# Low parts of split weights: an accumulating DMA onto the negated high parts in place of a subtraction on VectorE or GpSimd

## The chip, the core and the metric

The kernel runs as one program on one core of a Trainium2 chip. The metric is the device time of one execution in microseconds (us). Five engines work side by side, each through its own queue of instructions in order: TensorE (PE; its weight loads are shown as PEld), VectorE (DVE), ScalarE (ACT), GpSimd (POOL) and SyncE (SP). DMAs are issued from the queues of SP, ACT and POOL and are carried by 16 DMA engines, which all of them share.

## The reference, cut to what matters

The model is a trunk of four sublayers in each of two layers, on 512 tokens of 1024 features in float32. Everything that is heavy is a product of activations with a weight matrix from DRAM:

```
for i in range(DEPTH):                       # DEPTH = 2
    x = layer_norm(DN_ALPHA * x + 0.5 * swiglu_ffn(x, ffn1_wgu[i], ffn1_wd[i]), ...)
    mix = mlstm_mixer(...) if i % 2 == 0 else gmlp_mixer(...)
    x = layer_norm(DN_ALPHA * x + mix, ...)
    x = layer_norm(DN_ALPHA * x + 0.5 * swiglu_ffn(x, ffn2_wgu[i], ffn2_wd[i]), ...)
    ple = jax.nn.sigmoid(x @ ple_wg[i] + ple_bg[i]) * (p[i] @ ple_wp[i])
    x = layer_norm(DN_ALPHA * x + ple, ...)

def swiglu_ffn(x, w_gu, w_d):                # w_gu [1024, 2*2816], w_d [2816, 1024]
    g, u = jnp.split(x @ w_gu, 2, axis=-1)
    return (jax.nn.silu(g) * u) @ w_d
```

## The kernel before

Each float32 operand of a product is written as the sum of two float32r numbers of 12 significand bits, a high part and a low part. A product is then three matmuls (`mm3`, L150 to L154): high by high, high by low, low by high. Activations are split where they are made (`split`, L156 to L158, and `turn_x`).

Weights come in tiles of 128 partitions by 1024 elements, 512 KB each, 396 of them in one execution. The class `Weights` streams them in the order of use. `load` (L78) brings one or two tiles by a DMA from SP into one of three raw buffers (`wraw`, 1 MB each). `fill` takes the next tile in the order for which a pair of buffers is free, writes its high part `whi` with a ScalarE copy that rounds (L96), and its low part `wlo = wraw - whi` with a subtraction (L97) on VectorE, or on GpSimd where the caller asked for it (`low=pool`). `take` hands the next tile to a product; `release`, written where the last product of a tile is, frees the buffers and at once writes the splits of the tile that will take them. Held tiles (`later=True`) are freed by `refill`.

There are six pairs of split buffers ("main"), and in some stages four more ("rows"), so a tile's split stands some five or six tiles ahead of its use. In several places it stands closer: where four tiles are used in turn by every block of tokens (`up_tokens`: the values of the mLSTM, the second half of the gMLP's input, the gate of the input embedding, here called PLE), a group's tiles are all released within its last block of tokens, and the next group needs its own four within one block.

Tiles come in three forms. Most (for the FFN's first matrix, q, k, z and the gMLP's u) are 8 blocks of rows by 128 columns, so a tile's partition is 8 runs of 512 B in DRAM and, because two tiles share a raw buffer, in the raw buffer too. Tiles of the down projections are whole rows of 1024 elements; those of `up_tokens` are two rows of 512 elements.

The order of the work is written out by hand (`manual_schedule`): each engine runs its instructions in the order in which the code emits them, and waits by semaphores for its operands and for its output buffer. GpSimd's own work, beside the splits that it is given, is small: a power in each LayerNorm (L375), half of the norm's scale and shift (L381, L382), masks, and a power in the mLSTM (L730) and the gMLP (L836).

Of the kernel before, what the change touches and what calls it, by code (L numbers as in the profile page):

```python
# [9 lines left out]
F32 = mybir.dt.float32  # L10
F32R = mybir.dt.float32r
AF = mybir.ActivationFunctionType
OP = mybir.AluOpType
PSUM = bass.MemoryType.PSUM
DRAM = bass.MemoryType.DRAM

P = 128
# [20 lines left out]

# Weights are split on chip into two float32r parts (12 significand bits each, their sum is exact).
RAW_BUFS = 3  # L40
# [3 lines left out]
class Weights:  # L44
    """Streams weight tiles through SBUF in the order of use: a DMA brings one or two tiles, each of
    which is split into its high and low part ahead of its use, as soon as a tile is released."""

# [10 lines left out]
    def add(self, *loads, kind="main"):  # L58
        """Each (ap, views): ap [128, a, b] of DRAM, at most 2048 elements a partition; the views are
        the tiles in it. The tiles of several loads take turns."""  # L60
        first = len(self.loads)
        self.loads.extend(ap for ap, _ in loads)
        self.left.extend(len(views) for _, views in loads)
        for i in range(len(loads[0][1])):
            self.order.extend((first + j, views[i], kind) for j, (_, views) in enumerate(loads))
# [16 lines left out]
    def fill(self, most=1000, low=None):  # L82
        while most and self.next_split < len(self.order):
# [10 lines left out]
            for i in range(parts):  # L94
                s = slice(i * shape[1] // parts, (i + 1) * shape[1] // parts)
                self.nc.scalar.activation(hi[:, s], raw[:, s], AF.Copy)  # L96
                (low or self.nc.vector).tensor_sub(lo[:, s], raw[:, s], hi[:, s].bitcast(F32))  # L97
            self.ready.append((hi, lo))
# [12 lines left out]
    def release(self, n=1, kind="main", later=False, low=None):  # L111
        """The last products of n tiles are emitted. later: their successors' splits wait for refill().
        low: the engine for the low part."""
        if later:
            self.held.extend([kind] * n)
        else:
            self.free[kind] += n
            self.fill(low=low)
# [12 lines left out]
def hybrid_trunk(ctx: ExitStack, tc, x, p, ln_g, ln_b, ffn1_wgu, ffn1_wd, ffn2_wgu, ffn2_wd,  # L131
# [18 lines left out]
    def mm3(ps, st, mv, start, stop):  # L150
        """ps += st.T @ mv with both operands in two parts."""
        mm(ps, st[0], mv[0], start=start, stop=False)  # L152
        mm(ps, st[0], mv[1], start=False, stop=False)  # L153
        mm(ps, st[1], mv[0], start=False, stop=stop)  # L154
# [14 lines left out]
    def row_ap(src, offset, n):  # L169
        """n contiguous elements of DRAM on all partitions."""  # L170
        return bass.AP(tensor=src.tensor, offset=src.offset + offset, ap=[[0, P], [1, n]])

    # ---- the order of the weights
    W = Weights(nc, raw_pool, split_pool)
# [10 lines left out]
    def add_pairs(w, a0, b0):  # L185
        """Two tiles of columns from a0 and two from b0, in turns."""
        W.add((w_cols(w, a0), cols2), (w_cols(w, b0), cols2))
# [5 lines left out]
    def add_wide(w, c0, kind="main"):  # L193
        """Four tiles, each two blocks of rows of 512 columns."""
        for k in (0, 4):
            W.add((kp(w)[:, k:k + 4, c0:c0 + 512], half4), kind=kind)
# [60 lines left out]

    # ---- the input, by tokens and by features
    xt = act.tile([P, TB, D], F32, name="xt")
# [17 lines left out]
    def turn_x(t, bank=dn_bank, halves=(0, 1)):  # L277
        """A block of tokens by features, in two parts."""
        for g in halves:
# [7 lines left out]

    # ---- parameters by feature: one column for each block of 128 features
    NCOL = 160
# [33 lines left out]

    # both parts of the gates' weights side by side, the bias for the first
    G = 2 * HEADS
# [6 lines left out]
    def load_gates():  # L332
# [9 lines left out]
        vec.memset(all_ones, 1.0)  # L342
        # tri[s, t] = 1 for s <= t
        pool.affine_select(out=tri, in_=all_ones, pattern=[[1, P]], compare_op=OP.is_ge, fill=0.0, base=0,
# [6 lines left out]

    # ---- LayerNorm over the features, by tokens and in place
    class Norm:
# [8 lines left out]
        def stats(self, t, i, n):  # L362
            """Of the i-th of n parts of the features."""
            if i == 0:
                self.st[t] = small.tile([P, n, 6], F32, name="st", tag=f"st{n}")
            vec.bn_stats(self.st[t][:, i], xt[:, t, i * D // n:(i + 1) * D // n])  # L366

        def apply(self, t, shared=False):
            """shared: GpSimd takes a half of the features."""
            y = xt[:, t]  # L370
# [26 lines left out]

    # what is left of a norm, for the next stage to run between its first products
    hooks = []
# [13 lines left out]
    def down(hs, first, norm=None, kind="main", low=None):  # L413
        """Adds hs.T @ (the next tiles of weights) to the residual, a block of tokens after the other."""
        n = len(hs)
        ws = []
# [26 lines left out]
    def up(ps, w, t0=0, t1=SEQ, hooked=()):  # L443
        """ps = w.T @ x for some tokens, by features."""
        for kb in range(KB):
# [4 lines left out]
    def up_staged():  # L450
        """The same for three tiles of weights, by tokens as they come."""
        banks = [up_bank("sup") for _ in range(3)]
# [8 lines left out]
    def up_tokens(t, ws, ps, c=slice(0, 512), hook=None, release=None):  # L461
        """ps = x @ w for a block of tokens, with four tiles of two blocks of rows each."""
        for kb in range(KB):
# [10 lines left out]

    # ---- macaron half-step: x = LN(alpha x + 0.5 swiglu(x))
    def ffn(layer, k, prepare=None):
# [36 lines left out]

    # ---- mLSTM over the whole sequence: the state's sums written out
    def mlstm():
        b_in = ml_b_in
        with tc.tile_pool(name="ml", bufs=1) as mp:
            rows_d = dram.tile([HEADS, SEQ], F32, name="rows_d")
            # by tokens: i_s + (sum of log f from s to the end of the d-th block before the target's), exp(-m)
            reach = mp.tile([P, 4, TB, HEADS], F32, name="reach")  # L520
# [18 lines left out]
            def gate_logs():  # L539
# [7 lines left out]
                vec.tensor_add(fg, ps[:, :, HEADS:G], low[:, :, HEADS:])  # L547
                # log sigmoid(f) = min(f, 0) - log(1 + e), e = exp(-|f|); log(1 + e) = 2 atanh(e / (2 + e))
                vec.scalar_tensor_tensor(e, fg, -1.0, fg, op0=OP.mult, op1=OP.max)
# [13 lines left out]
            def gate_sums():  # L563
                """Sums of log f within a block of tokens (up to each token, and whole), the rows of i and log f."""
                ps = dn_bank("gsum")
# [20 lines left out]
            def gate_rows():  # L586
                """By target, for all sources alike: the sum of log f from its block's start less the maximum."""
                brow, mcol = up_bank("brow"), dn_bank("mcol")
# [14 lines left out]
            def project_qk(h):  # L603
                """q and k by features, after the convolution over tokens."""
                qh, ql = big("A", F32R, "qh"), big("B", F32R, "ql")
# [38 lines left out]
            def project_v(h, vb, between=()):  # L644
                """v by tokens, with two columns of ones between its halves."""
                ws = []
# [14 lines left out]
            def project_z(h, sz, i):  # L661
                """norm_g sigmoid(z), a block of features."""
                ps = up_bank("zps")
# [12 lines left out]
            def scores(h, qk, rt):  # L676
                """(q k) exp(...) by source, in blocks of sources."""
                qh, ql = qk
# [22 lines left out]
            def mix(h, ss, v):  # L701
                vh, vl = v
                hn = big("A", F32, "hn")
                for t in reversed(range(TB)):
                    bank = up_bank if t >= 2 else dn_bank
                    pa, pb = bank("nps"), bank("nps")
                    for j in range(t + 1):
# [8 lines left out]
                        mm(pb[:, :HV], sl[:, s], vh[:, j, HV + 2:], start=False, stop=last)  # L716
                    # h = num / max(|den|, exp(-m)); its LayerNorm from the sums of num
                    r = small.tile([P, 6], F32, name="hr", tag="hr")
# [60 lines left out]

    # ---- gMLP: gating by a product over the tokens of a block  # L780
    def gmlp():
        with tc.tile_pool(name="gm", bufs=1) as mp, tc.tile_pool(name="ghpool", bufs=4) as hpool:
            vf = mp.tile([P, TB, GW], F32, name="gvf")
            # both parts of a group's weights side by side
            wsp = mp.tile([P, GRP, 2, P], F32R, name="wsp")
# [6 lines left out]
            def spatial_weights():  # L792
# [3 lines left out]
                for a in range(2):  # L796
# [6 lines left out]
                    vec.tensor_sub(wsl[:, s], ps, wsh[:, s].bitcast(F32))  # L803
                # the later half of a block's tokens is hidden from the earlier
                vec.memset(wsh[64:128, :, 0:64].bitcast(F32), 0.0)
# [53 lines left out]
            def spatial(b, v):  # L859
                """The gate of a block of features: vn_g * P + (vn_b * rowsum(ws) + bs)."""  # L860
                vh, vl = v
# [44 lines left out]

    # ---- gated input embedding: x = LN(alpha x + sigmoid(x wg + bg) * (p wp))
    def ffn_ple(i, last):
# [116 lines left out]
```

## Time and profile before

| | |
|---|---|
| median of 2 runs | 2328.59 us (2328.36 to 2328.81) |
| span of the profiled execution | 2324.9 us, 3.7 us below that median |
| ACT busy | 699.2 us, 30% of the span |
| DMA, mean over the span | 98 GB/s |
| HBM read | 224.51 MB |
| weight loads of 1 MB from `ffn_wgu` | 80, median 5.8 us to landing |

The profile is of one execution. "Busy" is the time in which an engine had an instruction running. Groups of instructions are listed by source line with their count, total and mean time, and the idle time of their engine just before them with what ended it. The share of a DMA queue is the time of its packets as a share of 16 engines over the span.

### The profile page before, as it was taken

Reading aid. Unit: us, or ns where it says so; the run is one execution under the profiler, and the core shown is the slowest. Engines: PE = TensorE matmul, PEld = TensorE weight load, DVE = VectorE, ACT = ScalarE, POOL = GpSimd, SP = SyncE. Lnnn points to the kernel's source line nnn. Section 1 sums busy time; section 2 is a strip of 40 time slices with the busy share of each in tenths; the row PEclk is TensorE's granted clock in tenths of the full one; section 3 lists DMA queues with packets and bytes.
Section 4 is the critical chain, followed back from the end, with each engine's and each line's share of the span. In section 5 each row is a group of like instructions: output and inputs, shape, how many; then the busy total and the mean of one; then the engine's idle time right before and its main releaser. Section 6 shows DMA issues by size and latency. Waiting matters only on the chain. (4 is left out here: it accounts for less than half of the span.)

```text
span 2324.9 us, 25736 instructions
## 1 busy us (share of the span) xinstructions
PE 2286.6 (98%) x10814; PEld 1910.0 (82%) x10814; DVE 1250.3 (54%) x1753; ACT 699.2 (30%) x936; POOL 268.1 (12%) x187
## 2 busy tenths in 40 slices
PE   8999999999999999999999999999999999999998
PEld 7888888887878788888888888888888888888887
DVE  5433347686666753434477434336566584333467
ACT  4222222443534142222233222222333333222222
POOL 1000003122242400000021000002021230000022
PEclk9999999999999999999999999999999999999999
DMA  6333231132231233333222332231322234322411
GB/s 201 127 109 104 74 112 42 59 118 92 81 100 55 100 109 109 109 109 127 82 91 91 127 109 91 82 118 50 122 91 94 76 121 140 96 95 69 145 46 55
DMA packets 164140, 228.26 MB, mean 98 GB/s; under 512 B 4277, under 2 KB 130325, under 8 KB 164025
## 3 DMA queue, kind: packets, MB, share of 16 engines
q1 hardware_dynamic: 157120, 211.83, 27.7%
q10 hardware_dynamic: 6616, 14.69, 2.1%
q8 instruction: 84, 1.38, 0.2%
q14 instruction: 32, 0.25, 0.0%
q0 software_dynamic: 288, 0.12, 0.0%
HBM read 224.51 MB, written 2.11 MB: 97 GB/s over the span
## 5 line engine op out<-in xcount | busy, mean ns | idle before, releaser
L97 DVE TENSOR_TENSOR wlo<-wraw,whi 128x1024 fp32r<-128x1024 f32 (+1 forms) x342 | 412.8, 1232 | 355.2 <-ACT whi L96 352.4
L154 PE MATMUL fps<-xh,wlo 128*128 128x512 f32 x1312 | 510.9, 389 | 0.0
L153 PE MATMUL fps<-xl,whi 128*128 128x512 f32 x1312 | 510.8, 389 | 0.0
L152 PE MATMUL fps<-xh,whi 128*128 128x512 f32 x1312 | 510.6, 389 | 0.0
L96 ACT ACTIVATE whi<-wraw 128x1024 fp32r<-128x1024 f32 (+1 forms) x397 | 406.0, 1048 | 235.5 <-PE dps L154 181.9
L153 PE MATMUL dps<-wlo,hh 128*128 128x512 f32 x960 | 375.8, 391 | 6.5 <-DVE wlo L97 6.5
L154 PE MATMUL dps<-whi,hl 128*128 128x512 f32 x960 | 376.1, 392 | 2.7 <-DVE hl L158 2.7
L152 PE MATMUL dps<-whi,hh 128*128 128x512 f32 x960 | 377.4, 393 | 0.3 <-ACT hh L157 0.3
L153 PEld LDWEIGHTS fps<-xl,whi 128*128 128x128 f32 x1312 | 246.3, 188 | 51.5
L152 PEld LDWEIGHTS fps<-xh,whi 128*128 128x128 f32 x1312 | 246.3, 188 | 51.4
L154 PEld LDWEIGHTS fps<-xh,wlo 128*128 128x128 f32 x1312 | 246.3, 188 | 51.2
L396 DVE TENSOR_TENSOR xt<-xt,dps 128x512 f32<-128x512 f32 x208 | 141.1, 683 | 250.6 <-PE dps L154 250.4
L153 PEld LDWEIGHTS dps<-wlo,hh 128*128 128x128 f32 x960 | 180.3, 188 | 46.7 <-DVE wlo L97 8.3
L154 PEld LDWEIGHTS dps<-whi,hl 128*128 128x128 f32 x960 | 180.2, 188 | 42.7 <-DVE hl L158 3.6
L152 PEld LDWEIGHTS dps<-whi,hh 128*128 128x128 f32 x960 | 180.3, 188 | 38.8 <-ACT hh L157 0.5
L497 ACT ACTIVATE sg<-fps 128x512 f32<-128x512 f32 x80 | 47.4, 593 | 504.7 <-PE fps L154 504.7
L375 POOL TENSOR_TENSOR rs<-rs,eps_pow 128x1 f32<-128x1 f32 x32 | 21.1, 659 | 1519.7 <-DVE rs L374 1519.7
L97 POOL TENSOR_TENSOR wlo<-wraw,whi 128x1024 fp32r<-128x1024 f32 x55 | 143.3, 2614 | 260.4 <-ACT whi L96 229.4
L157 ACT ACTIVATE hh<-hf 128x512 fp32r<-128x512 f32 x88 | 55.7, 633 | 339.8 <-DVE hf L500 337.9
L500 DVE SCALAR_TENSOR_TENSOR hf<-sg,fps 128x512 f32<-128x512 f32 x84 | 57.6, 685 | 167.8 <-PE fps L154 167.8
L158 DVE TENSOR_TENSOR hl<-hf,hh 128x512 fp32r<-128x512 f32 x88 | 60.9, 692 | 61.5 <-ACT hh L157 61.5
L285 ACT ACTIVATE xh<-xps 128x512 fp32r<-128x512 f32 x64 | 37.4, 595 | 146.9 <-PE xps L283 146.9
(237 smaller groups left out, 2961.0 us busy)
## 6 DMA issues: line engine op xcount, KB each, us to landing
wraw<-in_ffn_wgu_dram SPq DMA_DIRECT2D x80, 1024.0 KB, 5.8
wraw<-in_ffn_wd_dram SPq DMA_DIRECT2D x44, 1024.0 KB, 4.9
wraw<-in_ml_w_in_dram SPq DMA_DIRECT2D x24, 1024.0 KB, 5.5
wraw<-in_gm_w_in_dram SPq DMA_DIRECT2D x15, 1024.0 KB, 5.7
wraw<-in_ml_w_out_dram SPq DMA_DIRECT2D x8, 1024.0 KB, 4.9
wraw<-in_ple_wg_dram SPq DMA_DIRECT2D x8, 1024.0 KB, 5.1
wraw<-in_gm_w_out_dram SPq DMA_DIRECT2D x8, 1024.0 KB, 4.9
wraw<-in_ffn_wgu_dram SPq DMA_DIRECT2D x15, 512.0 KB, 4.2
```

The source lines that it names most:

```text
L96: self.nc.scalar.activation(hi[:, s], raw[:, s], AF.Copy)
L97: (low or self.nc.vector).tensor_sub(lo[:, s], raw[:, s], hi[:, s].bitcast(F32))
L152: mm(ps, st[0], mv[0], start=start, stop=False)
L153: mm(ps, st[0], mv[1], start=False, stop=False)
L154: mm(ps, st[1], mv[0], start=False, stop=stop)
L157: sca.activation(hi, src, AF.Copy)
L158: vec.tensor_sub(lo, src, hi.bitcast(F32))
L285: sca.activation(xh[dst], ps, AF.Copy)
L375: pool.tensor_tensor(rs[:, 1:2], rs[:, 0:1], eps_pow, op=OP.pow)
L396: vec.tensor_add(dst, dst, ps)
L497: sca.activation(sg, pg, AF.Silu)
L500: vec.scalar_tensor_tensor(hf, sg, 0.5, pu, op0=OP.mult, op1=OP.mult)
```

## The change

The first two tiles are split as before. For every later tile the subtraction is gone. ScalarE copies the raw tile a second time, with a scale of -1, into `wlo`, so that `wlo` holds minus the rounded high part. Then GpSimd issues a DMA that adds the raw float32 tile onto `wlo`; the DMA reads the raw values, reads what is in `wlo`, adds, and writes `wlo`. For tiles with an even number the raw values are read from the raw buffer in SBUF; for tiles with an odd number they are read a second time from DRAM. The argument `low` no longer has an effect for these tiles. Comments and docstrings are removed as well, and the lines below the edit move down by five.

```
                 self.nc.scalar.activation(hi[:, s], raw[:, s], AF.Copy)
-                (low or self.nc.vector).tensor_sub(lo[:, s], raw[:, s], hi[:, s].bitcast(F32))
+                if self.next_split < 2:
+                    self.nc.vector.tensor_sub(lo[:, s], raw[:, s], hi[:, s].bitcast(F32))
+                else:
+                    self.nc.scalar.activation(lo[:, s], raw[:, s], AF.Copy, scale=-1.0)
+                    src = self.loads[j][view] if self.next_split % 2 else raw[:, s]
+                    self.nc.gpsimd.dma_start(lo[:, s], src, accum_op=OP.add)
```

394 of the 396 tiles take the new way. 214 of them have 8 runs of 512 B in a partition, the others one or two longer ones. Three places show what this does to the order on the engines; the numbers behind the names tell buffers apart.

ScalarE near the start, after the first tokens are turned (`xh`), before:

```order
L285 ACTIVATE xh_84<-xps_232 128x4x128
L96 ACTIVATE whi_251<-wraw_95 128x1024
L96 ACTIVATE whi_255<-wraw_129 128x1024
L96 ACTIVATE whi_259<-wraw_95 128x1024
L96 ACTIVATE whi_265<-wraw_129 128x1024
L96 ACTIVATE whi_271<-wraw_149 128x1024
```

and the same place in the changed kernel:

```order
L290 ACTIVATE xh_84<-xps_232 128x4x128
L96 ACTIVATE whi_251<-wraw_95 128x1024
L100 ACTIVATE wlo_252<-wraw_95 128x1024
L96 ACTIVATE whi_256<-wraw_129 128x1024
L100 ACTIVATE wlo_257<-wraw_129 128x1024
L96 ACTIVATE whi_261<-wraw_95 128x1024
L100 ACTIVATE wlo_262<-wraw_95 128x1024
```

Each high part is now followed by the negated copy, so a burst of splits is twice as long on ScalarE.

VectorE in the PLE of the first layer, where two buffers of weights and four of the second half's tiles come free together; `pg` is the gate's sum, the first work behind the splits, before:

```order
L286 TENSOR_TENSOR xl_85<-xps_8722,xh_84 128x4x128
L97 TENSOR_TENSOR wlo_8730<-wraw_8297,whi_8729 128x1024
L97 TENSOR_TENSOR wlo_8734<-wraw_8297,whi_8733 128x1024
L97 TENSOR_TENSOR wlo_8740<-wraw_8365,whi_8739 128x1024
L97 TENSOR_TENSOR wlo_8744<-wraw_8365,whi_8743 128x1024
L97 TENSOR_TENSOR wlo_8750<-wraw_8433,whi_8749 128x1024
L97 TENSOR_TENSOR wlo_8756<-wraw_8737,whi_8755 128x1024
L966 TENSOR_TENSOR pg_8790<-gps_8765,bgb_8634 128x512
```

and GpSimd at the same place in the changed kernel, between the last power of the norm before and the first of the norm behind:

```order
L380 TENSOR_TENSOR rs_8819<-rs_8819,eps_pow_102 128x1
L102 DMA wlo_8930<-wraw_8493 128x1024
L102 DMA wlo_8935<-in_ple_wg_dram 128x2x512
L102 DMA wlo_8942<-wraw_8563 128x1024
L102 DMA wlo_8947<-in_ple_wg_dram 128x2x512
L102 DMA wlo_8954<-wraw_8633 128x1024
L102 DMA wlo_8961<-in_ffn1_wgu_dram 128x8x128
L380 TENSOR_TENSOR rs_9036<-rs_9036,eps_pow_102 128x1
```

Six subtractions leave VectorE, and six DMA issues stand on GpSimd's queue ahead of the next norm's power.

SP's queue in the first FFN, where raw buffers are loaded, with what each issue waits for (DMAHW are earlier DMAs of SP, DMASW are DMAs of GpSimd), before:

```order
L78 DMA wraw<-in_ffn_wgu_dram 128x8x256 [waits DMAHW7_49,DVE_49]
L78 DMA wraw<-in_ffn_wgu_dram 128x8x256 [waits DMAHW3_49,DMAHW0_49,DVE_49]
L78 DMA wraw<-in_ffn_wgu_dram 128x8x256 [waits DMAHW1_49,DVE_49]
L78 DMA wraw<-in_ffn_wgu_dram 128x8x256 [waits DMAHW5_49,DMAHW2_49,DVE_49]
L78 DMA wraw<-in_ffn_wd_dram 128x2x1024 [waits DMAHW6_49,DMAHW3_49,DVE_49]
```

and in the changed kernel:

```order
L78 DMA wraw<-in_ffn_wgu_dram 128x8x256 [waits DMAHW0_49,Activation_49]
L78 DMA wraw<-in_ffn_wgu_dram 128x8x256 [waits DMAHW3_49,DMAHW7_49,DMASW3_49,DMASW1_49]
L78 DMA wraw<-in_ffn_wgu_dram 128x8x256 [waits DMAHW1_49,DMASW5_49,Activation_49]
L78 DMA wraw<-in_ffn_wgu_dram 128x8x256 [waits DMAHW2_49,DMASW7_49,DMAHW5_49,DMASW1_49,Activation_49]
L78 DMA wraw<-in_ffn_wd_dram 128x2x1024 [waits DMAHW6_49,DMAHW3_49,Activation_49]
```

A raw buffer was free once VectorE had subtracted; now it is free once ScalarE has copied and, where the tile's DMA reads the buffer, once that DMA has landed.

## The prediction

> **What bounds the kernel now.** I read the page's busy times first, then who waits for whom, then the busy times by stretch, and last the timeline at the places where a weight tile is split late.
>
> ```profile
> span 2324.9 us, 25736 instructions
> PE 2286.6 (98%) x10814; PEld 1910.0 (82%) x10814; DVE 1250.3 (54%) x1753; ACT 699.2 (30%) x936; POOL 268.1 (12%) x187
> L97 DVE TENSOR_TENSOR wlo<-wraw,whi 128x1024 fp32r<-128x1024 f32 (+1 forms) x342 | 412.8, 1232 | 355.2 <-ACT whi L96 352.4
> L96 ACT ACTIVATE whi<-wraw 128x1024 fp32r<-128x1024 f32 (+1 forms) x397 | 406.0, 1048 | 235.5 <-PE dps L154 181.9
> L97 POOL TENSOR_TENSOR wlo<-wraw,whi 128x1024 fp32r<-128x1024 f32 x55 | 143.3, 2614 | 260.4 <-ACT whi L96 229.4
> ```
>
> PE has work for 2286.6 of 2324.9 us: only 38 us could be won by any change that leaves the matmuls alone. The subtractions that the change removes (412.8 us on DVE, 143.3 us on POOL) lie on engines that are half idle or more. What PE waits for among them is in the view of waits:
>
> ```profile
> PE dps L153 <- DVE wlo L97: 6.5, 4, 1.8
> PE sup L154 <- DVE wlo L97: 0.8, 1, 0.8
> SPq L78 <- DVE wlo L97: 1782.7, 173, 53.3
> ```
>
> PE waits 7.3 us in all for low parts, and SP stands 1782.7 us waiting for raw buffers to come free: weights arrive far ahead, and the splits keep up. So the change can win almost nothing, and the question is whether the new way to a low part keeps up too: in rate, over a whole FFN, and in latency, where a tile is split shortly before its use.
>
> **The rate.** The third FFN has 66 tiles, and its stretch is this (time, then busy time of PE, PEld, DVE, ACT and POOL, the clock, DMA share and GB/s):
>
> ```profile
> 1250.00:1593.00 343.00, 343.00 (x1545) 284.95 (x1544) 147.44 (x166) 94.13 (x115) 3.89 (x3) 1.00 0.34 111
> q1 hardware_dynamic: 252, 0.97, 12.5%
> ```
>
> PE uses a tile in 343/66 = 5.2 us and never idles. The DMA engines spend 0.34 x 343 = 117 us, which is 1.77 us of all 16 engines on each tile of 512 KB. The second row is the queue of loads in a 20 us stretch with one burst of long rows: 0.97 MB for 2.5 us of all engines, or 1.35 us a tile. One pass of 512 KB thus costs 1.35 to 1.77 us. An accumulating DMA is nowhere in the trace. It cannot cost less than a plain pass, and by its work (it reads the raw values, reads `wlo`, writes `wlo`) I bound it at three passes. I take two, one for each operand read, because a plain pass already holds a read and a write side by side: 2.7 to 3.5 us. With the raw load, a tile then takes 4.05 to 5.3 us of the DMA engines against PE's 5.2 us. It fits, barely. I use 4.7 us as the spacing of low parts in a burst.
>
> The Trainium skill, "Collectives: The Full Stack", section "Why ReduceScatter is half of AllGather", says that an add in the DMA engines costs nothing by itself, and that the second source read halves the rate, from about 31 GB/s an engine. No run here shows it. By its figure, as an estimate, an accumulation of 512 KB takes 2.1 us and a tile 3.5 us, no FFN would be short of DMA, and the sum below would be about 2379 us instead of the forecast.
>
> **The change part by part.** ACT gets 394 more copies of 1.05 us (the row of L96 above), 413 us in all: 699 + 413 = 1112 us, 48% of the span. That is hidden in rate, but each negated copy stands behind its high part and delays it, as below. DVE loses 410 us, POOL loses 143 us of subtraction; nobody waits long for either, so I count 0 (at most the 7.3 us). POOL gets 394 DMA issues. The nearest rows are the loads that POOL issues at the start:
>
> ```profile
> 5.20 0.95 POOL L335 DMA_DIRECT2D graw<-in_ml_w_in_dram  x1
> graw<-in_ml_w_in_dram POOLq DMA_DIRECT2D x1, 32.0 KB, 7.0
> gbias<-in_ml_b_in_dram POOLq DMA_DIRECT2D x1, 0.0 KB, 5.1
> wraw<-in_ffn_wgu_dram SPq DMA_DIRECT2D x80, 1024.0 KB, 5.8
> wraw<-in_ffn_wgu_dram SPq DMA_DIRECT2D x15, 512.0 KB, 4.2
> ```
>
> `graw` has 1024 runs, as many as a tile of columns, and takes 0.95 us to issue. I take 1.0 us a tile, at most 1.9 if the second read is written as well: 394 to 750 us of 2325, hidden beside PE. What is queued behind an issue on POOL is the norm's power (L375). At the one stage end that matters (the last block of tokens of the mLSTM and gMLP) POOL does a subtraction of 2.6 us in the same place today, so 0.
>
> The landing time is what counts. 512 KB from SP land in 4.2 us; small loads from POOL took 5.1 to 7.0 us, among the start's other loads. I take 4.2 plus one more pass, 6.0 us; the ends are 4.2 (as a plain load) and 7.0 + 1.8 = 8.8. From the start of the high part to a usable low part: 2 x 1.05 + 1.0 + 6.0 = 9.1 us, where today it is 1.05 + 1.23 = 2.3 us. For most tiles 9.1 us is covered by the five tiles of 5.2 us that PE has in hand. The cover is thin in these places; each pair of rows is the high part's start and the first matmul that needs its low part:
>
> ```profile
> 20.09 5.80 ACT L96 ACTIVATE whi<-wraw 128x1024 fp32r<-128x1024 f32 x6
> 22.46 0.39 PE L154 MATMUL sup<-xh,wlo 128*128 128x256 f32 x1 [0.76 <-DVE wlo L97]
> 491.40 1.05 ACT L96 ACTIVATE whi<-wraw 128x1024 fp32r<-128x1024 f32 x1
> 495.78 0.39 PE L153 MATMUL vps<-wlo,xh 128*128 128x512 f32 x1
> 1188.27 4.84 ACT L96 ACTIVATE whi<-wraw 128x1024 fp32r<-128x1024 f32 x5
> 1193.24 0.40 PE L153 MATMUL gps<-wlo,xh 128*128 128x512 f32 x1
> 1194.65 0.39 PE L153 MATMUL gps<-wlo,xh 128*128 128x512 f32 x1
> 1234.58 1.05 ACT L96 ACTIVATE whi<-wraw 128x1024 fp32r<-128x1024 f32 x1
> 1240.93 0.28 PE L154 MATMUL sup<-xh,wlo 128*128 128x256 f32 x1
> 1624.30 1.06 ACT L96 ACTIVATE whi<-wraw 128x1024 fp32r<-128x1024 f32 x1
> 1625.66 1.06 ACT L96 ACTIVATE whi<-wraw 128x1024 fp32r<-128x1024 f32 x1 [0.30 <-PE gvps L154]
> 1631.13 0.39 PE L153 MATMUL gvps<-wlo,xh 128*128 128x512 f32 x1
> ```
>
> - Start, third tile: 20.09 + 9.1 = 29.2 against 22.46: 6.7 us.
> - Values of the mLSTM, fourth tile of the first head: 500.5 against 495.78: 4.7 us; two later heads have about 4 us more room: 0.6 each. Together 6 us.
> - PLE, second half of the gate: 1197.4 against 1193.24: 4.1 us; PE takes a new tile every 1.41 us there (1194.65 - 1193.24), and the next three low parts come 4.7 us apart: 3 x 3.3 = 9.9. Two layers: 28 us.
> - First FFN tile behind that PLE: 1243.7 against 1240.93: 3 us.
> - gMLP, the two tiles split in a group's last block of tokens: 1633.4 against 1631.13: 2.3 us, and 4.7 - 1.36 = 3.3 for the second. Three changes of group: 17 us.
>
> That is 61 us. On top comes the rate: 0 if a tile takes 4.05 us of DMA, and at 5.3 us 264 FFN tiles x 0.1 = 26 us, plus 28 us for the 16 loads of norm parameters (1.77 us each) that then find no gap. Because 214 of the accumulations are cut into runs of 512 B, I lean to the upper end and take 45 of these 54 us. Sum: 2324.9 + 61 + 45 = 2431; the median of the runs stands 3.7 us above the span: 2435 us.
>
> **The rivals.** *Three passes or more: DMA becomes the bound.* A tile takes 5.4 to 7.1 us of DMA. For: short runs, and a destination that must be read, changed and written. Against: nothing in the trace. Price: 264 FFN tiles x 0.2 to 1.9 us, at the middle 277 us; about 20 us in the gMLP (48 tiles in 300 us); the thin places with a chain of 10.6 and a spacing of 6.2 us cost 8 + 10 + 40 + 4 + 26 = 88 us. 2324.9 + 385 + 3.7 = 2714 us, from 2500 to 2960. PE would wait for low parts in the middle of each FFN.
>
> *The DMA is hidden: not slower.* One mechanism: an accumulation lands like a plain load (4.2 us) and takes one pass, so the chain is 7.3 us and the spacing ACT's 2.1 us. The thin places then cost 4.9 + 2.9 + 8.8 + 0.9 + 3.6 = 21 us: 2350 us. For: the DMA engines are 66% idle in the FFNs, and the accumulation is cut as finely as `graw`. Against: three times the memory traffic, and POOL's tiny load took 5.1 us to land. It decides as soon as the landing is under 5.3 us and the spacing under 3.5 us: the places then sum to about 42 us, under 2% of 2328.6.
>
> *POOL becomes the bound.* If an issue takes 6 us instead of 1.0, the FFNs run at 6 us a tile: 264 x 0.8 = 211 us, with the thin places about 2620 us. The `graw` row speaks against it.
>
> **How the numbers follow.** The forecast (2375 to 2500 us by itself) has 0.47, three passes or more 0.32, hidden 0.16, POOL 0.05. The range leaves out most of the hidden case below 2360 and the far end of the DMA bound above 2900, together under 0.2. 2% is about what a measurement of this kernel can tell from no change, 46.6 us: slower by more is every case but the hidden one, 0.84; same 0.15; faster 0.01, since PE leaves 38 us at most.
>
> **What would show it right or wrong.** Right: waits of PE for DMA into `wlo` at the start, in the PLEs and between the gMLP's groups, with FFN stretches near 343 us each; a DMA share of 0.8 to 1.0 in the FFNs; issues of `wlo` on POOL near 1 us and landings of 6 to 9 us. Wrong, on the slow side: FFN stretches of 400 us or more, landings over 15 us, or issues near 5 us. Wrong on the other side: landings near 4 us, a share near 0.65, and no wait of PE that is longer than 5 us.

## The result, and the profile after

| | before | changed |
|---|---|---|
| median of 2 runs each | 2328.59 us | 2456.66 us (2456.39 to 2456.93) |
| span of the profiled execution | 2324.9 us | 2455.2 us |
| mean granted clock of PE | 0.998 | 0.979 |

The ratio is 1.0549, with a 95% interval of 1.0519 to 1.058: slower by 128 us. From the page of the changed kernel: the span, the busy times, the queue of the accumulating DMAs (packets, MB, share of 16 engines), and the groups of the copies and of the issues (count, busy time, mean in ns, idle time before and what ended most of it).

```profile
span 2455.2 us, 26591 instructions
PE 2333.2 (95%) x10814; PEld 1928.1 (79%) x10814; DVE 782.2 (32%) x1414; ACT 1059.1 (43%) x1330; POOL 619.5 (25%) x526
q0 software_dynamic: 251840, 206.71, 58.3%
L96 ACT ACTIVATE whi<-wraw 128x1024 fp32r<-128x1024 f32 (+1 forms) x397 | 416.3, 1049 | 773.0 <-DMA wraw<-in_ffn_wgu_dram 513.5
L102 POOL DMA_DIRECT2D wlo<-wraw x197 | 250.5, 1281 | 714.7 <-ACT wlo L100 615.5
L100 ACT ACTIVATE wlo<-wraw 128x1024 fp32r<-128x1024 f32 x394 | 411.6, 1045 | 0.0
L102 POOL DMA_DIRECT2D wlo<-in_ffn_wgu_dram x87 | 134.2, 1542 | 658.4 <-ACT wlo L100 643.2
wlo<-wraw POOLq DMA_DIRECT2D x197, 512.0 KB, 10.2
wlo<-in_ffn_wgu_dram POOLq DMA_DIRECT2D x87, 512.0 KB, 8.7
wraw<-in_ffn_wgu_dram SPq DMA_DIRECT2D x80, 1024.0 KB, 11.6
```

PE, which was busy for all but 38.3 us, now stands 122.0 us (2455.2 - 2333.2): 83.7 us more. And its busy time itself has grown by 46.6 us, for the same 10814 matmuls. These two make up the 130.3 us between the spans. ACT's copies came as costed (1.045 us each), and ACT, DVE and POOL are idle for more than half of the time: none of them has become the bound. The last three rows are times to landing. A low part lands in about 9 to 10 us in these rows (13.3 us for the odd tiles of the down projections), and a raw load of 1 MB, which took 5.8 us, takes 11.6.

What PE and ACT waited for, from the view of waits (total, times, longest):

```profile
PE dps L157 <- ACT hh L162: 31.7, 15, 8.6
PE dps L158 <- DMA wlo<-wraw: 13.2, 6, 3.8
PE sup L159 <- DMA wlo<-wraw: 11.8, 2, 8.8
PE gvps L158 <- DMA wlo<-in_gm_w_in_dram: 11.4, 3, 4.6
PE gps L158 <- DMA wlo<-wraw: 6.9, 4, 2.9
PE gps L158 <- DMA wlo<-in_ple_wg_dram: 6.3, 3, 3.2
PE qps L159 <- DMA wlo<-in_ml_w_in_dram: 4.6, 1, 4.6
ACT whi L96 <- DMA wraw<-in_ffn_wgu_dram: 513.5, 58, 15.5
```

Low parts that land late stop PE in the mLSTM (`qps`, and `dps` with a low part), at the start (`sup`), in the gMLP (`gvps`) and the PLE (`gps`). The largest row is of another kind: PE waits for `hh`, the split hidden activations of an FFN, which come from ACT, and ACT waits half a millisecond for raw weights. The two kernels run the same matmuls in the same order, so each matmul's start in one trace can be set against the same matmul's start in the other, and the lag read wherever it grows. Worked out so, over both layers (us; the times are those of the profile before):

| place | predicted | measured |
|---|---|---|
| start, to 50 | 6.7 | 11.0 |
| mLSTM, 455 to 800 | 6 | 32.9 |
| start of the second FFN of each layer, 836 to 850 and 1918 to 1935 | 0 | 21.8 |
| PLE, 1180 to 1250 and 2262 to 2285 | 28 + 3 | 19.2 |
| first FFN of the second layer, first down projections, 1262 to 1280 | 0 | 10.2 |
| gMLP, 1593 to 1850 | 17 | 22.1 |
| everything else, the long stretches of the FFNs above all | 45 | 12.6 |

The sum comes near (106 against 130) and the parts do not. The experiments follow the rows of this table.

### The profile page after: what moved, and what is told of

Read it like the earlier page. It is cut to its first block, busy times and chain, and to the rows that moved or that the text cites. A ratio compares the mean times of both kernels' runs of the same rounds, so it can differ in the third digit from the quotient of the medians.

```text
span 2455.2 us, 26591 instructions
## 1 busy us (share of the span) xinstructions
PE 2333.2 (95%) x10814; PEld 1928.1 (79%) x10814; DVE 782.2 (32%) x1414; ACT 1059.1 (43%) x1330; POOL 619.5 (25%) x526
## 3 DMA queue, kind: packets, MB, share of 16 engines
q0 software_dynamic: 251840, 206.71, 58.3%
q1 hardware_dynamic: 157120, 211.83, 26.5%
## 4 chain that ended last, share of the span: by engine, by line
PE 56%; DMA 19%; issue 10%; DVE 6%; ACT 5%; POOL 3%; SPq 0%; POOLq 0%; ACTq 0%; DVEq 0%
DMA wraw<-in_ffn_wgu_dram 7%; PE fps L158 7%; PE dps L157 7%; PE fps L157 7%; PE fps L159 7%; PE dps L159 7%; PE dps L158 7%; DMA wlo<-wraw 6%; POOL wlo L102 2%; DMA wlo<-in_ml_w_out_dram 2%; ACT wlo L100 1%; DMA wlo<-in_ml_w_in_dram 1%; ACT whi L96 1%; DMA wlo<-in_gm_w_in_dram 1%; DVE xt L392 1%
## 5 line engine op out<-in xcount | busy, mean ns | idle before, releaser
L96 ACT ACTIVATE whi<-wraw 128x1024 fp32r<-128x1024 f32 (+1 forms) x397 | 416.3, 1049 | 773.0 <-DMA wraw<-in_ffn_wgu_dram 513.5
L102 POOL DMA_DIRECT2D wlo<-wraw x197 | 250.5, 1281 | 714.7 <-ACT wlo L100 615.5
L157 PE MATMUL dps<-whi,hh 128*128 128x512 f32 x960 | 385.6, 402 | 31.8 <-ACT hh L162 31.7
L100 ACT ACTIVATE wlo<-wraw 128x1024 fp32r<-128x1024 f32 x394 | 411.6, 1045 | 0.0
L158 PE MATMUL dps<-wlo,hh 128*128 128x512 f32 x960 | 383.3, 399 | 17.8 <-DMA wlo<-wraw 13.2
L159 PE MATMUL dps<-whi,hl 128*128 128x512 f32 x960 | 383.0, 399 | 0.0
L102 POOL DMA_DIRECT2D wlo<-in_ffn_wgu_dram x87 | 134.2, 1542 | 658.4 <-ACT wlo L100 643.2
L159 PE MATMUL sup<-xh,wlo 128*128 128x256 f32 x240 | 70.4, 293 | 11.8 <-DMA wlo<-wraw 11.8
## 6 DMA issues: line engine op xcount, KB each, us to landing
wlo<-wraw POOLq DMA_DIRECT2D x197, 512.0 KB, 10.2
wraw<-in_ffn_wgu_dram SPq DMA_DIRECT2D x80, 1024.0 KB, 11.6
wlo<-in_ffn_wd_dram POOLq DMA_DIRECT2D x44, 512.0 KB, 13.3
```

What stands on the lines that cost most here:

```text
L100: self.nc.scalar.activation(lo[:, s], raw[:, s], AF.Copy, scale=-1.0)
L102: self.nc.gpsimd.dma_start(lo[:, s], src, accum_op=OP.add)
```

## The experiments

Twelve kernels, against 2326.9 to 2328.6 us for the kernel before, measured beside them. Three theories stood at first. A: low parts land late where a tile is split shortly before use. B: an accumulation that reads the raw buffer holds it until it has landed, so the next raw weights come late, ACT stands on them in its fixed order, and what is queued behind on ACT (the split of `h`) comes late too. C: the DMA engines are full, and the FFNs run at their rate.

**Nobody reads the low part.** All DMAs and copies stay; the product takes the high part in its place.

```
-            self.ready.append((hi, lo))
+            self.ready.append((hi, hi) if self.next_split >= 2 else (hi, lo))
```

> The third product of mm3 reads the high part again instead of the low part, from the third tile on, so the computation is changed; the negated copies, the accumulating DMAs and all buffers stay. No matmul waits for an accumulation any more. Theory A (PE stalls because low parts land late at the thin places, 63 us of waits in the changed kernel, and each stall is followed by some us at half clock): the time falls by 63 to 100 us, to 2355 to 2395 us. Theory B (the loss is that raw tiles come late, ScalarE stands on them and its other work, the split of h, comes late): the time falls by under 30 us and stays above 2425 us. Rival C (the DMA engines are short of rate): stays within 15 us of 2457 us.

2391.0 us, ratio 1.0266 (1.0247 to 1.0285): 65.7 us go when nobody waits for low parts. The rest of the loss stays, and in it the wait for `hh`, 31.7 us in the change. From the view of waits of this kernel (`xt` is the norm's result, which PE turns for the next product):

```profile
PE dps L157 <- ACT hh L162: 39.9, 18, 7.8
PE xps L288 <- DVE xt L392: 12.5, 4, 9.7
```

Both are longer than in the change: other waits come up where those for low parts were.

**All accumulations read DRAM**, so none of them holds a raw buffer.

```
-                    src = self.loads[j][view] if self.next_split % 2 else raw[:, s]
+                    src = self.loads[j][view]
```

> Every accumulation reads its raw values from DRAM, none from the raw buffer, so a raw buffer is free once ScalarE has made its two copies. Theory B (raw buffers are held until an accumulation has landed, so raw loads are late): ScalarE's waits for raw tiles of the FFN fall from 513 us to under 100 us, the waits of PE for the split of h (31.7 us) go, and the time falls by 30 to 60 us, to 2395 to 2425 us. Rival C (rate): 103 MB more from HBM cost time, 2457 us or more. Theory A alone: within 10 us of 2457 us, since the landings stay about 9 us.

2422.46 us, ratio 1.0397 (1.0377 to 1.0418): 34 us come from the hold. The expected fall of ACT's wait for raw weights under 100 us did not come, but PE's wait for `hh` has left the list. PE's longest wait is now this, with ACT's row below it in the view of waits:

```profile
PE gvps L158 <- DMA wlo<-in_gm_w_in_dram: 19.9, 6, 6.0
ACT whi L96 <- DMA wraw<-in_ffn_wgu_dram: 317.6, 47, 14.1
```

ACT's wait in itself costs nothing; it costs where PE has nothing left that ACT has made.

**Both edits at once.**

> Both edits at once: the third product reads the high part again (computation changed), and all accumulations read DRAM. A and B together explain the loss if this returns to 2328 to 2345 us. Rival C: the DMA work is all still there, so a time above 2380 us would be its mark.

2340.9 us, ratio 1.0053 (1.0034 to 1.0072). On its page the queue of the accumulations is as busy as in the change, and PE nearly as little idle as before:

```profile
PE 2292.4 (98%) x10814; PEld 1913.4 (82%) x10814; DVE 782.0 (33%) x1414; ACT 1057.0 (45%) x1330; POOL 630.5 (27%) x526
q0 software_dynamic: 262080, 206.71, 59.9%
```

So C falls: the same bytes, copies and issues cost 12 us against the kernel before, and 23 us against the next run, which has the copies alone, when nobody waits for what they make and they hold no raw buffer.

**The accumulation left out**, copies kept:

```
-                    src = self.loads[j][view] if self.next_split % 2 else raw[:, s]
-                    self.nc.gpsimd.dma_start(lo[:, s], src, accum_op=OP.add)
```

> The negated copy stays and the accumulating DMA is left out, so the low part is minus the high part and the computation is changed. What is left is the cost of ScalarE's 394 further copies. Theories A, B and C all put nothing on ScalarE itself: 2322 to 2335 us. If ScalarE's copies are the loss, it stays above 2400 us.

2317.62 us, ratio 0.9953 (0.9939 to 0.9968), below the expected 2322. ACT's 394 copies are hidden, and taking DVE and POOL out of the split is worth 11 us, a little more than the 7.3 us that the prediction had as the most.

**All accumulations read the raw buffer** (`src = raw[:, s]`): the hold doubled.

> Every accumulation reads the raw buffer in SBUF, so each raw buffer is held until both its accumulations have landed, and 103 MB less are read from HBM than in the changed kernel. Theory B (held raw buffers make raw loads and the split of h late): slower than 2457 us by 20 us or more, 2477 to 2520 us, with waits of PE for the split of h well above 31.7 us. Rival C (DMA rate, HBM traffic): 2457 us or less.

2480.22 us, ratio 1.0657 (1.0642 to 1.0671), slower than the changed kernel by 24 us, as B has it. The wait for `hh` did not grow as expected; the loss went to the gate's `sg`, another operand that ACT makes, as the view of waits has it:

```profile
PE fps L157 <- ACT sg L502: 24.3, 4, 6.8
PE dps L157 <- ACT hh L162: 25.7, 8, 4.4
```

**Thin tiles by subtraction.** The 58 tiles that are split shortly before use are subtracted on DVE; 336 accumulate as in the change.

```
-                if self.next_split < 2:
+                if self.next_split < 2 or self.next_split in THIN:
...
+THIN = {2, 3, 4, 72, 73, 77, 84, 85, 89, 90, 96, ...}
```

> 58 further tiles, those whose low part PE read less than 20 us after the start of the high part in the trace before, are split by a subtraction on VectorE again; the other 336 keep the accumulation, half of them from the raw buffer. Theory A (late landings at the thin places): the waits of PE for accumulations fall from 63 us to under 10 us and the time by 50 to 80 us, to 2375 to 2405 us, near the 2391 us of the run in which PE reads no accumulation. Theory B alone or rival C (rate): a fall of no more than 58 of 394 parts, to about 2440 us.

2358.39 us, ratio 1.0133 (1.0116 to 1.015). That is 98 us less than the change, more than the 66 of A alone, which suggests that the bursts of these tiles are also where raw buffers were held. In the view of waits that for `hh` is almost gone, though ACT waits for raw weights nearly as long as in the change.

```profile
PE dps L161 <- ACT hh L166: 6.9, 12, 1.4
ACT whi L100 <- DMA wraw<-in_ffn_wgu_dram: 481.5, 59, 15.3
```

**The same, and the 336 others from DRAM.**

> The same 58 tiles by subtraction, and all 336 accumulations read DRAM. A and B together are the loss: 2328 to 2350 us, with nothing left out of the computation this time. If part of the gain of the run in which PE reads no low part came from the computation that it leaves out, this stays above 2370 us.

2338.78 us, ratio 1.0046 (1.0031 to 1.0061): accumulating for 336 tiles of 396 costs about 10 us when the thin tiles are kept out and no raw buffer is held.

**What a halt of PE costs beside its own length.** PE's busy time had grown with the count of its halts. So the kernel before was given twelve halts, by matmuls that wait for a chain of additions on POOL, in two lengths:

```
+            halt = rows.tile([P, 256], F32, name="halt", tag="halt", bufs=1)
...
+                    if b == 1 and c in (1, 2, 3):
+                        pool.tensor_add(halt, hf[:, :256], hf[:, :256])
+                        for _ in range(3):
+                            pool.tensor_add(halt, halt, hf[:, :256])
+                        nc.tensor.transpose(up_bank("hps")[:, :P], halt[:, :P], ident)
```

> The kernel before, with 12 added halts of PE: in three chunks of each FFN a transpose waits for a chain of 4 additions on GpSimd that starts from the product's result, about 5 us of idle PE each. Idle time alone: 12 x 5 = 60 us more than before. If PE also runs at half clock for 3.4 us or more behind each halt, another 1.7 us or more for each: 80 us or more, and PE's busy time grows by 20 us or more. If halts of 5 us are too short for it, PE's busy time stays at 2287 us.

The second kernel has `range(10)`.

> The same with chains of 11 additions, about 11 us of idle PE each. Idle time alone: 12 x 11 = 132 us more than before. With a stretch at half clock behind each halt: 155 to 175 us, and PE's busy time 20 to 45 us above 2287 us.

2429.29 us, ratio 1.0432 (1.0412 to 1.0453), and 2526.23 us, ratio 1.0849 (1.0827 to 1.087). Both kinds of halt were longer than expected, the long ones by 3 us. The busy times on the page of the short halts, and PE's wait for the twelve in the view of waits:

```profile
PE 2316.0 (95%) x10826; PEld 1927.0 (79%) x10826; DVE 1267.2 (52%) x1753; ACT 699.1 (29%) x936; POOL 326.1 (13%) x235
```

```profile
PE hps L511 <- POOL halt L510: 73.0, 12, 6.1
```

The same two of the long halts:

```profile
PE 2316.3 (92%) x10826; PEld 1928.1 (76%) x10826; DVE 1279.4 (51%) x1753; ACT 698.8 (28%) x936; POOL 422.4 (17%) x319
```

```profile
PE hps L511 <- POOL halt L510: 171.3, 12, 14.3
```

Against 2286.6 us before, busy time rises by 29.4 and 29.7 us: 2.5 us for each halt, whether it lasted 6.1 or 14.3 us. The added transposes take 0.13 us of it each (from the start of one to the start of the next matmul), which leaves 2.3 us. Wait and growth make 102.4 and 201.0 us, and the spans are longer by 102.9 and 199.2. The windows show where (time, busy time of PE, PEld, DVE, ACT, POOL, the granted clock, DMA share, GB/s). Behind a short halt, the first 4 us of work and the next 4:

```profile
78.00:82.00 4.00, 3.92 (x10) 3.16 (x11) 3.38 (x3) 0.12 (x1) 0.03 (x1) 0.50 0.94 313
82.00:86.00 4.00, 4.00 (x18) 3.29 (x18) 0.00 (x0) 0.15 (x1) 0.00 (x0) 0.99 1.06 359
```

A long halt, the 3.1 us behind it, and the next 5:

```profile
72.60:86.90 14.30, 0.03 (x1) 0.00 (x0) 9.45 (x7) 5.36 (x6) 12.62 (x11) 0.64 0.78 252
86.90:90.00 3.10, 3.10 (x8) 2.52 (x9) 0.00 (x0) 0.00 (x0) 0.00 (x0) 0.50 0.26 92
90.00:95.00 5.00, 5.00 (x22) 4.09 (x22) 0.00 (x0) 0.62 (x2) 0.00 (x0) 0.97 0.00 0
```

After a halt PE resumes at half clock (10 matmuls in 4 us against 18) and is back at full clock some microseconds later. The Trainium skill, "TensorE: Matmul & The Clock Gate", section "Part 1: The HAM clock gate", gives this rule: an idle window of about 3.4 us halves the array's clock, and about as long a busy one restores it. The traces agree roughly. In their clock record the clock halves 2.0 to 5.3 us after a halt begins and is restored 2.8 to 6.1 us after it ends, 4.4 us on average behind the short halts and 4.6 behind the long ones. An estimate by that page is half of 3.4, 1.7 us lost a halt; half of the measured stretches is 2.2 and 2.3 us.

**GpSimd's queue.** In the mLSTM the changed kernel's trace shows something that A had not named. From the timelines of POOL, ACT and PE (start, duration, and in brackets the idle time before and what ended it); `hr` is the power in the norm of a head's output:

```profile
558.60 0.56 POOL L735 TENSOR_TENSOR hr<-hr,eps_pow 128x1 f32<-128x1 f32 x1 [3.02 <-DVE hr L734]
...
569.21 0.55 POOL L735 TENSOR_TENSOR hr<-hr,eps_pow 128x1 f32<-128x1 f32 x1 [2.98 <-DVE hr L734]
569.83 0.90 POOL L102 DMA_DIRECT2D wlo<-wraw  x1
570.47 1.13 POOL L102 DMA_DIRECT2D wlo<-in_ml_w_out_dram  x1
571.07 1.42 POOL L102 DMA_DIRECT2D wlo<-wraw  x1
...
557.14 1.05 ACT L100 ACTIVATE wlo<-wraw 128x1024 fp32r<-128x1024 f32 x1
...
575.34 0.80 PE L158 MATMUL dps<-wlo,hh 128*128 128x512 f32 x1 [3.20 <-DMA wlo<-wraw]
```

ACT has written the negated copy at 558.2, and POOL issues the accumulation at 569.83: 11.6 us later, behind four powers that each wait 3 us for DVE. Then five issues start within 2.4 us. To tell GpSimd's order from the burst itself, the 16 powers were taken off GpSimd (VectorE takes a reciprocal, and the square root is left out), and the same was done to the kernel before:

```
-                    pool.tensor_tensor(r[:, 4:5], r[:, 3:4], eps_pow, op=OP.pow)
+                    vec.reciprocal(r[:, 4:5], r[:, 3:4])
```

> The changed kernel, with the mLSTM's 16 powers (L735) taken off GpSimd: VectorE computes a reciprocal in their place (the square root is left out). In the trace of the changed kernel GpSimd reaches the issues of a head's low parts only behind these powers, up to 11 us after ScalarE has written the negated copy (issue at 569.83, copy done at 558.2). If GpSimd's order is what makes the mLSTM late, the issues follow their copies within 2 us, PE's waits for low parts in the mLSTM (26.5 us in all with qps, vps and dps) fall under 10 us, and the time falls by 15 to 32 us, to 2425 to 2442 us. If the burst of six accumulations is slow for its own sake (DMA share 1.17 in that place), the issues move but the landings stay long, the waits stay above 20 us, and the time stays at 2450 to 2460 us.

> Control: the kernel before with the same edit. Low parts do not pass through GpSimd's queue there except where the tile is split on GpSimd; both theories expect 2320 to 2332 us.

2416.08 us, ratio 1.0381 (1.0365 to 1.0397), below the expected 2425; and 2322.2 us, ratio 0.9978 (0.9968 to 0.9987), for the kernel before. So 40.6 us less in the one and 4.7 us less in the other, net 36 us: as much as the held raw buffers. GpSimd's order makes low parts late, so these 36 us are a part of the 65.7 us of theory A, not a loss beside them. (The DMA share of 1.17 in the expectation belongs to the stretch from 485 to 500; around the burst shown, from 569 to 577, it is 0.76.) In the timeline of the edited kernel the same issue goes out right behind its copy (the copy ends at 544.71, the issue starts at 545.00):

```profile
543.65 1.06 ACT L100 ACTIVATE wlo<-wraw 128x1024 fp32r<-128x1024 f32 x1
...
545.00 0.89 POOL L102 DMA_DIRECT2D wlo<-wraw  x1 [2.93 <-PE nps L718]
```

PE's waits in the whole mLSTM of this kernel, 455 to 805, are led by these two, where 26.5 us of waits for low parts stood in the changed kernel:

```profile
PE dps L157 <- ACT hh L162: 2.4, 1, 2.4
PE vps L158 <- DMA wlo<-in_ml_w_in_dram: 1.3, 2, 1.0
```

**A version that might have been faster than before.** Since 7.3 us of waits for subtractions stood in the kernel before, most of them in the mLSTM, its four splits behind each head were shared, two on DVE and two on POOL (`refill` hands `most` on to `fill`):

```
-                W.refill(4)
+                W.refill(4, most=2)
+                W.fill(low=pool)
```

> The kernel before, with one edit: of the four tiles that the mLSTM splits together behind its mix, VectorE subtracts two and GpSimd two. The run without accumulation came out 11 us under the kernel before, 8 us of it in the products that follow these splits, where PE waits 6.5 us for VectorE's low parts. If that wait and the half clock behind it are the 8 us: 2317 to 2324 us. If the gain came from VectorE's lighter load as a whole: within 2 us of the kernel before.

2336.78 us, ratio 1.0035 (1.0022 to 1.0049): a miss, slower by 8. PE's wait for low parts there rose from 6.5 to 11.5 us in the view of waits:

```profile
PE dps L153 <- DVE wlo L97: 11.5, 6, 2.8
```

No version that computes the reference beat the kernel before. A fourth raw buffer, which would show the hold in another way, wasn't tried.

**The runs by place.** The lag behind the kernel before (us), worked out as in the table above:

| kernel | start | mLSTM | 2nd FFNs' start | PLE | 1st FFN, layer 2 | gMLP | rest |
|---|---|---|---|---|---|---|---|
| changed | 11.0 | 32.9 | 21.8 | 19.2 | 10.2 | 22.1 | 12.6 |
| low part not read | -1.7 | -2.9 | 20.6 | 10.2 | 10.1 | 2.6 | 26.3 |
| all from DRAM | 7.7 | 29.5 | 2.8 | 18.9 | 0.9 | 28.8 | 11.2 |
| both of these | -1.2 | -8.9 | 3.6 | 6.3 | 4.9 | 0.0 | 12.4 |
| no power on GpSimd | 10.5 | -7.0 | 20.5 | 20.7 | 10.8 | 22.7 | 12.7 |
| all from the buffer | 8.6 | 31.5 | 23.0 | 19.4 | 10.7 | 11.9 | 49.4 |
| thin tiles subtracted | -0.9 | 8.3 | 0.3 | 1.1 | 0.1 | 0.0 | 18.9 |

Each cause has its places. Late landings: start, gMLP and half of the PLE (they go when nobody reads the low part). GpSimd's order: the mLSTM, all of it. The held raw buffer: the FFN starts, 32 us, of which 31 stay when the low part isn't read and 4 when nothing holds a raw buffer. Each entry contains the half-clock time behind its halts. The rest, spread over the long stretches, was not followed to its causes.

The causes also hide one another. Where the low part isn't read, 11.0 us come back between 50 and 100, counted under the rest, with one wait of 7.8 us for `hh`. The half of the PLE that stays there is a wait of 9.7 us for `xt`: ACT stands 10.9 us on a raw tile of the next FFN, and the PLE's gate `pg` is queued behind that split. So one edit alone brings less than its cause is worth, and both together bring 116 us, more than 66 + 34. The source cuts both ways: in the gMLP the lag is 11.9 us when all accumulations read the buffer, 22.1 when half of them do, and 28.8 when all read DRAM.

One FFN start, from the timelines of ACT and PE in the changed kernel:

```profile
883.10 1.06 ACT L96 ACTIVATE whi<-wraw 128x1024 fp32r<-128x1024 f32 x1 [5.94 <-DMA wraw<-in_ffn_wgu_dram]
...
895.37 1.06 ACT L96 ACTIVATE whi<-wraw 128x1024 fp32r<-128x1024 f32 x1 [9.75 <-DMA wraw<-in_ffn_wgu_dram]
...
898.23 0.60 ACT L502 ACTIVATE sg<-sup 128x512 f32<-128x512 f32 x1
...
900.60 0.63 ACT L162 ACTIVATE hh<-hf 128x512 fp32r<-128x512 f32 x1
901.29 0.79 PE L157 MATMUL dps<-whi,hh 128*128 128x512 f32 x1 [8.13 <-ACT hh L162]
```

and from its windows, the halt and its end:

```profile
895.00:898.40 3.40, 0.00 (x0) 0.00 (x0) 0.51 (x1) 3.03 (x5) 0.73 (x1) 0.66 0.96 236
898.40:901.80 3.40, 0.51 (x1) 0.50 (x2) 1.90 (x4) 3.40 (x5) 1.46 (x2) 0.50 0.62 78
```

ACT stands 9.75 us on a split whose raw tile is not there. The gate `sg`, on which `hf`, then `hh` and PE's next matmul hang, is queued behind that split, though it needs none of its weights. PE stops for 8.13 us, and starts again at half clock.

## Why the prediction was right and wrong

- **PE is the bound, little can be won, the change loses.** Right: with no accumulation at all the gain is 11 us.
- **ACT's copies are hidden.** Right (no_accumulate). One thing was missing: *what is queued behind the copies and the splits on ACT*. In the prediction a split was late only for its own tile. Where a raw tile is late, ACT's order makes `sg` and `hh` late as well.
- **Two passes of DMA.** Right in kind. 58.3% of 16 engines over 2455.2 us, by 394, is 3.63 us of all engines for an accumulation; the prediction had 2.7 to 3.5. That is 2.05 of the prediction's plain passes of 1.77 us, or 2.2 of the 1.64 us that the loads' own queue spends on a tile in this run (26.5% of the span, by 396). The share counts packet times, which can overlap (it reads 1.06 in one row above), so 3.63 us is an upper bound. The Trainium skill's rule, "Collectives: The Full Stack", section "Why ReduceScatter is half of AllGather", that the second source read halves the rate, agrees with the ratio of 2.05 to 2.2. The estimate from its figure, 2.1 us an accumulation, does not agree: 3.63 us were measured.
- **The rate term of 45 us.** Wrong: everything outside the listed places lags by 12.6 us. The stretch of the first FFN in the changed kernel:

```profile
50.00:393.00 343.00, 341.41 (x1504) 279.89 (x1503) 71.56 (x109) 146.10 (x172) 90.09 (x70) 1.00 1.02 202
```

  The DMA share is 1.02, where it was 0.30 before, and PE is busy for 341.41 of 343 us, just as it was before in this window. The matmuls that took 340 us before (from 50 to 390) took 3.4 us longer. Full DMA engines by themselves cost this stretch 1%. What the step had to ask as well was how long each transfer *holds* what it reads: the prediction counted the bytes of the second read and not the raw buffer that stays taken. It named SP's 1782.7 us of waiting for raw buffers as a sign of slack; the slack was in time, not in buffers.
- **POOL's issues, 1.0 us, at most 1.9, hidden.** The size was right (1.54 us for tiles of columns, about 0.9 for rows). The step "At the one stage end that matters (...) POOL does a subtraction of 2.6 us in the same place today, so 0" failed: it asked what stands behind an issue on POOL, and not what an issue stands behind. Net of the control, 36 us.
- **The landing, 6.0 us (4.2 to 8.8).** Mis-sized: the medians above are 8.7 to 10.2 us, and a load of raw weights takes twice its time as well. The shortest accumulation landed in 4.5 us, near the 4.2 us of a plain load, the longest in 26.5, so much of the landing looks like waiting among other transfers; no run separates that from the second read. At the start and in the gMLP the lag is 33.1 us against 24; in the PLE, where it was listed tile by tile, 19.2 against 28 + 3.
- **The clock.** Not in the prediction. A granted clock of 0.979 is 103 us at half clock (2 x 0.021 x 2455), against about 9 before. PE stands in a part of it; by the clock record it is busy in 72 us, which costs 36. PE's busy time rises by 46.6 us, more than a third of the loss; the other 10 us of it were not followed.
- **The rivals.** Three passes: no FFN stretch of 400 us. Hidden DMA: landings of 4 us were not seen. POOL as the bound: it is idle for three quarters of the time, and yet its queue, by order and not by rate, cost 36 us.

So 2435 us came near 2456.7 in part by luck, by errors that cancel: 32 us too many for the rate (45 against the 12.6 of everything else) and 12 too many in the PLE with its next tile, against 27 too few in the mLSTM, 32 in the FFN starts, which were not on the list, and 9 at the start and in the gMLP.

## What to carry to other kernels

When an instruction is turned into a DMA, ask three things besides its bytes: what the issue stands behind on its queue, which buffers the transfer holds until it lands, and what is queued behind the engine that waits for those buffers. A halt of TensorE of 6 us or more cost its length and over 2 us of slow clock behind it here, so count halts as well as their lengths. Split tiles that are used soon on an engine (here 58 of 396), and let the DMAs of the others read a source that nobody waits to reuse: the two together brought the loss from 128 us to 10.

## What the runs showed of the hardware

- The slow clock behind a halt cost about the same, 2.3 us, for halts of 6.1 us and of 14.3 us.
- When several issues of accumulations go out together, their recorded times grow and overlap: in the rows from 569.83 on, GpSimd's DMA instructions take 0.90, 1.13 and 1.42 us, where one by itself took 0.89 us, while their starts stay 0.6 us apart.
- With the DMA share at 1.02 against 0.30 before, the same matmuls of the first FFN took 343.4 us against 340.0: full DMA engines cost 1% where tiles are split five ahead of their use.
